# Second layer: normalised activations stored token tile by token tile, and a wider slot for the last head pair's projections

## The chip, the cores and the metric

The kernel runs on one core of one Trainium2 chip. The metric is the device time of one launch in microseconds; the time given for a kernel is the median over its runs. Engines are called as the profile calls them: PE is TensorE's matmul stream (PEld its weight loads), DVE is VectorE, ACT is ScalarE, POOL is GpSimd and SP is SyncE, which here issues nearly all DMAs.

## What is computed

Two transformer-like layers over 1024 latent tokens and 256 context tokens, width 1024. The first layer is grouped-query attention with rotary positions. The second, which the change touches, is neighbourhood attention: each query sees an 8 x 16 window of the 16 x 64 grid plus all context tokens. Cut to the second layer, the reference is:

```
hx = rms_norm(x, g) * (1 + scale_x) + shift_x        # 1024 latent tokens
hc = rms_norm(ctx, g) * (1 + scale_c) + shift_c      # 256 context tokens
q, k, v, z = split(hx @ w_in)                        # 16 heads of 64
kc, vc = split(hc @ w_in[:, k and v columns])
s = [q . k(window) / 8 + bias,  q . kc / 8]
p = softmax(s)
y = (p . [v(window), vc] * silu(z)) @ w_out
x = x + gate * y
return rms_norm(x, final_g)
```

Activations and weights are each held as a pair of half-precision tiles, a high part and a low part (`hb_hi`, `hb_lo`; `wb[u][0]`, `wb[u][1]`), and every projection is the sum of three products: high by high, high by low, low by high.

## The kernel before, in words

**Tiling.** Tokens come in ten tiles of 128: tiles 0 to 7 are latent, 8 and 9 context. The contraction over 1024 channels is eight chunks of 128, counted by `kt`. The 16 heads are worked on as eight pairs, u = 0 to 7.

**From the first to the second layer.** `a_out(t)` is the first layer's output projection of token tile t (matmuls into `poa`, line 1233) and adds it to the residual `x1s[t]`, called x10 to x17 in the listings. `b_ln(t)` calls `ln_tile`: sum of squares on ACT (`xj`, line 614), inverse root on POOL (`rs_ln`, line 607), scaling of the tile on DVE (line 616), eight transposes on PE into `plb{t}0` and `plb{t}1` (line 621), scale and shift on ACT into `tf` (line 625), and on DVE the copy to `hb_hi` (line 628) and the remainder to `hb_lo` (line 629). Both have the shape [128, 8 chunks, 1280 tokens]; one call of lines 628 and 629 writes four chunks of 128 tokens each.

**Per head pair.** `b_load(u)` fetches and splits the weights (`wb`). `b_qk(u)` makes five blocks of Q or K: 24 matmuls each into `pb{u}{which}{first token}` (which is 0 for Q and 1 for K), with weights as the stationary operand and 512 or 256 tokens of `hb` as the moving one (line 1319). ACT and DVE then evict them to `bq` and `bk` (lines 1332 to 1337). `b_vz(u)` makes V and the gate z for two token tiles at a time in `pvz{u}{0..4}`, with `hb` as the stationary operand (lines 1351 and 1354; `pvz{u}4` is the context's V), evicted to `bv` and `bsz`. `b_att(u)` computes window scores (`bsn{u}{head}{tile}`, lines 1382 and 1383) and context scores (`bsc`), adds the bias table `tb` and takes the maximum on DVE (line 1402), four exponentials per query tile on ACT (lines 1420 to 1423), the low part on POOL or DVE, a DMA transpose to `bpht`, and then the product with V into `bpv` (lines 1431 and 1433). `b_out(t)` is the final output projection (`pob{t}{half}`, line 1523), whose weights are `wob`.

**PSUM.** `pb`, `pvz` and the first four tiles' `pob` share two banks (tag `pj`), so a block can start when the last but one has been evicted. Window scores share two banks (`st`) with the later `pob`.

**What sets the order.** The program is first written out by `timeline`, which merges generators by a start and an end on a common axis: attention of pair u has the slot u to u + 1, the projections of pair u + 1 the slot u + BP0 to u + BP1, that is u to u + 0.95. Then `Planner` reorders every engine's instructions: it builds a dependency graph, runs a list schedule with its own costs, derives due times and reschedules, and the order it ends with is fixed per engine. To find what depends on what it does not use exact access patterns. `box` reduces each operand to one interval of elements per partition, from its first to its last element:

```
for s, c in ap[1:]:
    if s >= 0:
        ext += s * (c - 1)
return t, p0, p0 + ap[0][1] - 1, f0 + lo, f0 + ext, False
```

With [128, 8, 1280], the write of tile 6 into chunks 0 to 3 is the interval from element 768 to 3 x 1280 + 895, which holds the elements of tiles 0 to 3 in chunks 1, 2 and 3 as well.

Of the kernel before, what the change touches and what calls it, by code (L numbers as in the profile page):

```python
# [13 lines left out]
F16 = mybir.dt.float16  # L14
BF16 = mybir.dt.bfloat16
AF = mybir.ActivationFunctionType
ALU = mybir.AluOpType
# [4 lines left out]
P = 128  # L22
D = 1024
KT = D // P
NX = 8
NC = 2
NT = NX + NC
TOK = NT * P
# [10 lines left out]
BP0, BP1 = 0, 0.95  # L39
# [415 lines left out]
def timeline(items):  # L455

    live = [[g, float(a), (float(b) - a) / tot, 0.0] for g, a, b, tot in items]
    while live:
        it = min(live, key=lambda e: e[1] + e[2] * e[3])
        try:  # L460
            c = next(it[0])
            it[3] += c
            yield c
        except StopIteration:
            live.remove(it)


def once(f):
    f()
    yield 1.0  # L470
# [8 lines left out]
def trunk_kernel(ctx, tc, x, cx, cc, norm_g, b_cols, sel_c, w_mod, b_mod, a_w_in, a_qg, a_kg, a_w_out,  # L479
                 b_w_in, rpb, b_w_out, fin_g, cos_t, sin_t, mask_q, out):  # L480
    nc = tc.nc
    V, S, G, T, DM = nc.vector, nc.scalar, nc.gpsimd, nc.tensor, nc.sync
# [6 lines left out]
    def ps_pj(name, dt=F32, shape=(P, 512)):  # L489
        return psum.tile(list(shape), dt, name=name, tag="pj", bufs=2)  # L490

    def ps_mx(name, dt=F32, shape=(P, 512)):
        return psum.tile(list(shape), dt, name=name, tag="mx", bufs=2)
# [109 lines left out]
    def rstd_from(pool, ss, n, mul, add, tag):  # L603
        ms = pool.tile([P, 8], F32, name="ms_" + tag, tag="ms" + tag, bufs=2)
        V.tensor_scalar(ms[:, 0:n], ss, mul, add, op0=ALU.mult, op1=ALU.add)
        rs = pool.tile([P, 8], F32, name="rs_" + tag, tag="rs" + tag, bufs=2)
        G.tensor_tensor(rs[:, 0:n], ms[:, 0:n], mhalf[:, 0:n], op=ALU.pow)
        return rs

    def ln_tile(pool, xt, l, s, hi, lo, c0, nm):  # L610

        jk = pool.tile([P, D], BF16, name="xj" + nm, tag="xj", bufs=1)
        ss = pool.tile([P, 1], F32, name="lss" + nm, tag="lss", bufs=2)
        S.activation(jk, xt, AF.Square, accum_out=ss)
        rs = rstd_from(pool, ss, 1, 1.0 / D, EPS, "ln")
        V.tensor_scalar_mul(xt, xt, rs[:, 0:1])
        for hf in range(2):
            ps = ps_mx(f"pl{nm}{hf}", shape=(P, 4, P))
            for j in range(4):
                kt = hf * 4 + j  # L620
                T.transpose(ps[:, j, :], xt[:, kt * P:(kt + 1) * P], idf)
            tf = pool.tile([P, 4, P], F32, name=f"tf{nm}{hf}", tag="tf", bufs=2)
            for j in range(4):
                kt = hf * 4 + j
                S.activation(tf[:, j, :], ps[:, j, :], AF.Identity, scale=acol[l][:, kt, s:s + 1],
                             bias=scol[l][:, kt, s:s + 1])
            k4 = slice(hf * 4, hf * 4 + 4)
            V.tensor_copy(hi[:, k4, c0:c0 + P], tf)
            V.tensor_tensor(lo[:, k4, c0:c0 + P], tf, hi[:, k4, c0:c0 + P], op=ALU.subtract)
            yield 450  # L630

    def load_w(wt, src_ap, kt0, nk, width, nm):
# [244 lines left out]
    NPAIR = NH // 2  # L877
# [308 lines left out]
    items = a_proj(0, -first)  # L1186
# [17 lines left out]
    gts, x1s, ops = {}, {}, {}  # L1204
# [47 lines left out]


    bpool = ctx.enter_context(tc.tile_pool(name="bpool", bufs=1))
    hb_hi = bpool.tile([P, KT, TOK], F16, name="hb_hi")
    hb_lo = bpool.tile([P, KT, TOK], F16, name="hb_lo")
    tc.swap_default_side()
    lnpool = ExitStack()
    lnp = lnpool.enter_context(tc.tile_pool(name="lnpool", bufs=1))
    tc.swap_default_side()  # L1260

    def b_ln(t):
        yield from ln_tile(lnp, x1s[t], 1, 0 if t < NX else 1, hb_hi, hb_lo, t * P, f"b{t}")


    bq = ctx.enter_context(tc.tile_pool(name="bq", bufs=2))
# [6 lines left out]
    for r in range(GR):  # L1273
        a = bass.AP(rpb.tensor, rpb.offset + 15 - r, [[31 * 31, NH], [31, 31], [1, GR]])
# [7 lines left out]
    hb = (hb_hi, hb_lo)  # L1282
# [23 lines left out]
    def b_qk(u):  # L1306
        wt = wb[u]
        q1 = bq.tile([P, 2, NX * P], F16, name=f"bq1{u}", tag="q1")
        k1_ = bq.tile([P, 2, TOK], F16, name=f"bk1{u}", tag="k1")
        q2 = q2z[u % 2]  # L1310
        v1_ = bq.tile([P, NT, 2, P], F16, name=f"bv1{u}", tag="v1")
        sz = bq.tile([P, NX, P], F32, name=f"bsz{u}", tag="sz")
        bpairs[u] = (q1, q2, k1_, v1_, sz)
        for which, c0, n in ((0, 0, 512), (1, 0, 512), (1, 1024, 256), (0, 512, 512), (1, 512, 512)):
            ps = ps_pj(f"pb{u}{which}{c0}")
            m = 0
            for kt in range(KT):
                for a, b in ((0, 0), (0, 1), (1, 0)):
                    T.matmul(ps[:, 0:n], wt[a][:, kt, which * P:(which + 1) * P], hb[b][:, kt, c0:c0 + n],  # L1319
                             start=m == 0, stop=m == 3 * KT - 1)  # L1320
                    m += 1
                    if m % 3 == 0:
                        yield 640 * n / 512


            for i in range(2):
                own, oth = slice(i * 64, i * 64 + 64), slice(64 - i * 64, 128 - i * 64)
                src = ps[own, 0:n]
                cs = slice(c0, c0 + n)
                if which == 0:  # L1330
                    sc = HD ** -0.5 / WS
                    S.activation(q1[own, i, cs], src, AF.Copy, scale=sc)
                    V.scalar_tensor_tensor(q2[own, i, cs], src, sc, q1[own, i, cs], op0=ALU.mult, op1=ALU.subtract)
                    V.tensor_copy(q1[oth, i, cs], q1[own, i, cs])
                else:
                    S.activation(k1_[own, i, cs], src, AF.Copy, scale=1.0 / WS)
                    V.scalar_tensor_tensor(k1_[oth, i, cs], src, 1.0 / WS, k1_[own, i, cs], op0=ALU.mult,  # L1337
                                           op1=ALU.subtract)

    def b_vz(u):  # L1340
        wt = wb[u]
        v1_, sz = bpairs[u][3:5]
        for b in range(NT // 2):
            ps = ps_pj(f"pvz{u}{b}", shape=(P, 2, 2, P))
            for j in range(2):
                t = 2 * b + j
                m = 0
                for kt in range(KT):
                    for a, w in ((0, 0), (0, 1), (1, 0)):
                        if b < NX // 2:  # L1350
                            T.matmul(ps[:, :, j, :], hb[a][:, kt, t * P:(t + 1) * P], wt[w][:, kt, 256:512],  # L1351
                                     start=m == 0, stop=m == 3 * KT - 1)
                        else:
                            T.matmul(ps[:, 0, j, :], hb[a][:, kt, t * P:(t + 1) * P], wt[w][:, kt, 256:384],  # L1354
                                     start=m == 0, stop=m == 3 * KT - 1)
                        m += 1
                        if m % 3 == 0:
                            yield 320
            for j in range(2):
                vv = ps[:, 0, j].rearrange("p (h d) -> p h d", d=HD)  # L1360
                S.copy(v1_[:, 2 * b + j, :, 0:HD], vv)
                V.tensor_tensor(v1_[:, 2 * b + j, :, HD:P], vv, v1_[:, 2 * b + j, :, 0:HD], op=ALU.subtract)
            if b < NX // 2:
                th = bq.tile([P, 2 * P], F32, name=f"bth{u}{b}", tag="th", bufs=1)
                zf = ps[:, 1].rearrange("p t f -> p (t f)")
                S.activation(th, zf, AF.Tanh, scale=0.5 / WS)
                V.scalar_tensor_tensor(sz[:, 2 * b:2 * b + 2].rearrange("p t f -> p (t f)"), th, 1.0, zf,
                                       op0=ALU.add, op1=ALU.mult)
# [90 lines left out]
    C_BP, C_BA = 23040 + 25600, 8 * 1890 + 500  # L1459

    def b_proj(u):
        return timeline([(b_qk(u), 0, 0.6, 23040), (b_vz(u), 0.3, 1, 25600)])

    def steps(txt):
        for step in txt.split():
# [3 lines left out]
            else:  # L1469
# [4 lines left out]
    run_all(steps("l0 o8 l1 o9 l2 o4 l3 l8 o50 l9 o60 l4 o70"))  # L1474
    items = [(steps("o51 o61 l5 o71 l6 l7"), 0, 0.8, 5120 * 3 + 450 * 6), (b_load(0), 0.05, 0.6, 8),
             (b_qk(0), 0.85, 1.8, 23040)]
    run_all(timeline(items))
    lnpool.close()
# [8 lines left out]
    for h in range(2):  # L1487
        b_table(h)
    run_all(timeline([(b_vz(0), 0, 1, 25600), (b_load(1), 0, 0.5, 8)]))
    items = []  # L1490
    for u in range(NPAIR):
        items.append((b_att(u), u, u + 1, C_BA))
        if u + 1 < NPAIR:
            items.append((b_proj(u + 1), u + BP0, u + BP1, C_BP))
            for i in range(2):
                items.append((once(lambda h=2 * (u + 1) + i: b_table(h)), u + (0.76, 1.1)[i], u + 2, 1))
        if u + 2 < NPAIR:
            items.append((b_load(u + 2), u + 0.5, u + 0.95, 8))
# [112 lines left out]
```

## Time and profile before

| | |
|---|---|
| median of 3 runs | 1415.17 us (1411.48 to 1416.53) |
| the profiled execution's own time | 1411.77 us |
| its span, first to last instruction | 1410.0 us |
| PE busy | 1352.2 us, 96% of the span |
| DVE, ACT, POOL busy | 988.8, 957.4, 661.7 us |
| mean granted TensorE clock | 0.995 |
| second layer's first projection matmul (`pb`) | 798.2 us |
| second layer's first V and z matmul (`pvz`) | 830.5 us |
| first output projection matmul (`pob`) | 1295.5 us |

A row of the timeline reads: start in us, duration, engine, line, operation, output <- inputs, shapes, count of merged instructions, and in brackets how long the engine had been idle and what released it. Names there leave out the trailing numbers that the listings below have. Matmuls are pipelined: a 512-column matmul is shown with 0.38 us, but the next one starts about 0.22 us after it. A row of the windows reads: the stretch, its length, then busy us and count of PE, PEld, DVE, ACT and POOL, the granted clock, the DMA engines' mean busy share and GB/s.

### The profile page before, as it was taken

How to read it: one execution, taken by the hardware profiler on the slowest of the kernel's cores; microseconds unless marked ns; L12 is line 12 of the kernel's file. 1: busy time of each engine (PE TensorE's matmuls, PEld its weight loads, DVE VectorE, ACT ScalarE, POOL GpSimd, SP SyncE). 2: the span in 40 equal slices, each digit the busy share in tenths (PEclk: the TensorE clock that was granted, in tenths of full speed). 3: DMA queues.
4: the chain of work that ended last, by engine and by line, in shares of the span. 5: the costliest groups of instructions: out<-in, count | busy, mean ns of one | idle time of the engine just before them, and what ended most of it. 6: DMA issues, size and time to landing. Idle time of an engine off the chain costs nothing.

```text
span 1410.0 us, 35562 instructions
## 1 busy us (share of the span) xinstructions
PE 1352.2 (96%) x13458; PEld 941.4 (67%) x13458; DVE 988.8 (70%) x2564; ACT 957.4 (68%) x2354; POOL 661.7 (47%) x907
## 2 busy tenths in 40 slices
PE   5899999999999999999999899999999999999897
PEld 2457777777777777776555466767777776767443
DVE  3696887878898767688234735786777867687833
ACT  2553889898978787788634625677777867777821
POOL 2322678786877686678852201323222222223332
PEclk9999999999999999999999999999999999999999
DMA  9843567888866222245023414566756767577932
GB/s 262 241 130 94 97 119 148 142 162 164 151 126 125 50 75 50 68 118 166 23 90 105 143 36 113 93 144 133 128 113 121 145 106 160 97 152 139 190 110 105
DMA packets 412403, 173.98 MB, mean 123 GB/s; under 512 B 319012, under 2 KB 391364, under 8 KB 412232
## 3 DMA queue, kind: packets, MB, share of 16 engines
q1 hardware_dynamic: 411656, 171.68, 55.3%
q8 instruction: 105, 1.72, 0.5%
q14 instruction: 66, 0.54, 0.1%
q10 hardware_dynamic: 576, 0.03, 0.0%
HBM read 85.65 MB, written 12.06 MB: 69 GB/s over the span
## 4 chain that ended last, share of the span: by engine, by line
PE 75%; DVE 8%; ACT 7%; DMA 5%; issue 2%; POOL 2%; SPq 0%; DVEq 0%; POOLq 0%; ACTq 0%
PE pvz L1351 12%; PE pa L914 11%; PE pb L1319 9%; PE poa L1233 7%; PE pob L1523 5%; PE st L1141 3%; PE st L1140 3%; PE pkv L800 3%; DMA qpp<-qpp 3%; PE pm L944 2%; PE pv L1012 2%; PE pv L1013 2%; PE pv L1011 2%; PE bpv L1431 1%; PE pvz L1354 1%
## 5 line engine op out<-in xcount | busy, mean ns | idle before, releaser
L1005 POOL TENSOR_TENSOR pl<-pf,ph 128x256 f16<-128x256 f32 x400 | 283.5, 731 | 72.0 <-ACT pf L1127 54.1
L1005 POOL TENSOR_TENSOR bph<-bpf,bph 128x256 f16<-128x256 f32 (+1 forms) x128 | 100.9, 799 | 339.8 <-ACT bpf L1422 285.5
L914 PE MATMUL pa<-wa,x 128*128 128x256 f16 x1536 | 225.3, 274 | 3.1 <-DVE q16q L730 2.9
L1319 PE MATMUL pb<-hb_hi,wb 128*128 128x512 f16 (+1 forms) x640 | 193.8, 359 | 0.0
L1125 ACT ACTIVATE ph<-st 128x512 f16<-128x512 f32 x240 | 143.9, 602 | 64.1 <-PE st L1141 58.4
L1351 PE MATMUL pvz<-wb,hb_hi 128*128 128x256 f16 x1024 | 173.5, 273 | 4.5 <-DVE bk L1337 3.9
L914 PEld LDWEIGHTS <-x 128*128 128x128 f16 x1536 | 140.1, 98 | 37.0 <-DVE q16q L730 2.8
L945 DVE TENSOR_REDUCE mxp<-pm 128x1 f32<-128x512 f32 x192 | 128.6, 683 | 34.9 <-PE pm L944 34.1
L1127 ACT ACTIVATE pf<-st 128x512 f32<-128x512 f32 x240 | 144.4, 604 | 0.4
L1319 PEld LDWEIGHTS <-wb 128*128 128x128 f16 x960 | 92.9, 98 | 72.4 <-issue 1.1
L1351 PE MATMUL pvz<-wb,hb_lo 128*128 128x256 f16 x512 | 139.5, 273 | 0.0
L1012 PE MATMUL pv<-v,ph 128*128 128x64 f16 x960 | 123.5, 195 | 0.0
L1011 PE MATMUL pv<-v,ph 128*128 128x65 f16 x960 | 122.7, 193 | 0.0
L1013 PE MATMUL pv<-v,pl 128*128 128x65 f16 x960 | 121.3, 192 | 0.3 <-POOL pl L1005 0.3
L1351 PEld LDWEIGHTS <-hb_hi 128*128 128x128 f16 x1024 | 98.7, 98 | 25.3 <-issue 6.6
L1319 PE MATMUL pb<-hb_lo,wb 128*128 128x512 f16 (+1 forms) x320 | 114.7, 359 | 0.0
L1005 POOL TENSOR_TENSOR qpp<-qpf,qpp 128x256 f16<-128x256 f32 (+1 forms) x158 | 91.8, 605 | 42.7 <-ACT qpf L1083 38.1
L1011 PEld LDWEIGHTS <-ph 128*128 128x128 f16 x960 | 90.9, 97 | 21.4 <-issue 0.4
L1012 PEld LDWEIGHTS <-ph 128*128 128x128 f16 x960 | 90.5, 97 | 16.4
L1013 PEld LDWEIGHTS <-pl 128*128 128x128 f16 x960 | 91.1, 99 | 7.8 <-POOL pl L1005 1.0
L1233 PE MATMUL poa<-woa,oa 128*128 128x512 f16 x384 | 92.0, 379 | 0.0
L1140 PE MATMUL st<-q,k 128*128 128x512 f16 x240 | 90.7, 379 | 0.8 <-ACT pf L1127 0.6
(266 smaller groups left out, 3691.1 us busy)
## 6 DMA issues: line engine op xcount, KB each, us to landing
wg<-in_w_mod SPq DMA_DIRECT2D x64, 256.0 KB, 3.4
wsb<-in_b_w_in SPq DMA_DIRECT2D x64, 256.0 KB, 3.5
wm<-in_w_mod SPq DMA_DIRECT2D x32, 256.0 KB, 5.1
wsa<-in_a_w_in SPq DMA_DIRECT2D x64, 128.0 KB, 2.6
xstage<-in_x SPq DMA_DIRECT2D x8, 512.0 KB, 8.1
wsoa<-in_a_w_out SPq DMA_DIRECT2D x16, 256.0 KB, 2.8
x<-in_x SPq DMA_DIRECT2D x8, 512.0 KB
x_d<-x SPq DMA_DIRECT2D x8, 512.0 KB, 3.8
```

Of the source, the lines that this page charges most:

```text
L914: T.matmul(ps[:, :, i, :], hA(a, kt, t), wt[w][:, kt, :], start=n == 0, stop=n == 3 * KT - 1)
L945: V.tensor_reduce(mxs[i][:, t, ch:ch + 1], pm, axis=AX.X, op=ALU.max)
L1005: G.tensor_tensor(lo[:, c], p32[:, c], hi[:, c], op=ALU.subtract)
L1011: T.matmul(pv[:, t, :], hi[:, c], v[:, 0:65], start=first and t == 0, stop=False)
L1012: T.matmul(pv[:, t, 0:HD], hi[:, c], v[:, 65:129], start=False, stop=False)
L1013: T.matmul(pv[:, t, :], lo[:, c], v[:, 0:65], start=False, stop=last and t == n - 1)
L1125: S.activation(ph, st, AF.Exp)
L1127: S.activation(p32, st, AF.Exp)
L1140: T.matmul(so, k1[:, g, kc], q1[:, :, i, :], start=True, stop=False)
L1233: T.matmul(ps, lhs(a, kt), w[b][:, kt, :], start=n == 0, stop=n == 3 * KT - 1)
L1319: T.matmul(ps[:, 0:n], wt[a][:, kt, which * P:(which + 1) * P], hb[b][:, kt, c0:c0 + n], start=m == 0, stop=m == 3 * KT - 1)
L1351: T.matmul(ps[:, :, j, :], hb[a][:, kt, t * P:(t + 1) * P], wt[w][:, kt, 256:512], start=m == 0, stop=m == 3 * KT - 1)
```

## The change

Two edits. The first turns `hb_hi` and `hb_lo` from [128, chunk, token] into [128, token tile, chunk, 128 tokens]. `ln_tile` now gets one tile's block and writes four chunks that lie side by side. `b_qk` reads four (or two) tiles at one chunk, that is runs of 128 elements, 1024 elements apart, and its PSUM output is viewed in the same way; `b_vz` reads one tile at one chunk, as before. The number of instructions and the elements of each stay as they were. The second edit makes the slot of the last pair's projections, which are merged with the attention of pair 6, longer by 0.3: from 6 to 7.25 instead of 6 to 6.95.

```
-    def ln_tile(pool, xt, l, s, hi, lo, c0, nm):
+    def ln_tile(pool, xt, l, s, hi, lo, nm):
...
-            V.tensor_copy(hi[:, k4, c0:c0 + P], tf)
-            V.tensor_tensor(lo[:, k4, c0:c0 + P], tf, hi[:, k4, c0:c0 + P], op=ALU.subtract)
+            V.tensor_copy(hi[:, k4], tf)
+            V.tensor_tensor(lo[:, k4], tf, hi[:, k4], op=ALU.subtract)
...
-    hb_hi = bpool.tile([P, KT, TOK], F16, name="hb_hi")
-    hb_lo = bpool.tile([P, KT, TOK], F16, name="hb_lo")
+    hb_hi = bpool.tile([P, NT, KT, P], F16, name="hb_hi")
+    hb_lo = bpool.tile([P, NT, KT, P], F16, name="hb_lo")
...
-                    T.matmul(ps[:, 0:n], wt[a][:, kt, which * P:(which + 1) * P], hb[b][:, kt, c0:c0 + n],
+                    T.matmul(ps[:, 0:n].rearrange("p (t q) -> p t q", q=P), wt[a][:, kt, which * P:(which + 1) * P],
+                             hb[b][:, c0 // P:(c0 + n) // P, kt],
                              start=m == 0, stop=m == 3 * KT - 1)
...
-                            T.matmul(ps[:, :, j, :], hb[a][:, kt, t * P:(t + 1) * P], wt[w][:, kt, 256:512],
+                            T.matmul(ps[:, :, j, :], hb[a][:, t, kt], wt[w][:, kt, 256:512],
...
-            items.append((b_proj(u + 1), u + BP0, u + BP1, C_BP))
+            items.append((b_proj(u + 1), u + BP0, u + BP1 + 0.3 * (u == NPAIR - 2), C_BP))
```

Since the planner's intervals change with the layout, the order of instructions changes too. Up to about 775 us of the profile no row of any engine moves. Lines from 1320 on have a number higher by one after the change.

The first place is PE at the passage between the layers. `poa71` is the first layer's last output block; `pb000` and `pb010` are the first Q and K block of pair 0, `plb60` to `plb71` the transposes of normalised tiles 6 and 7. Before:

```order
L1319 MATMUL pb010_14642<-hb_hi_13857,wb00_14419 128x512
L1319 LDWEIGHTS wb00_14419
L1319 MATMUL pb010_14642<-hb_lo_13858,wb00_14419 128x512
L1319 LDWEIGHTS wb01_14420
L1319 MATMUL pb010_14642<-hb_hi_13857,wb01_14420 128x512
L621 MATMUL plb60_14551<-idf_66,x16_14298 128x128 x4
L621 MATMUL plb61_14563<-idf_66,x16_14298 128x128 x4
L621 MATMUL plb70_14583<-idf_66,x17_14360 128x128 x4
L621 MATMUL plb71_14595<-idf_66,x17_14360 128x128 x4
L1319 LDWEIGHTS wb00_14419
L1319 MATMUL pb000_14611<-hb_hi_13857,wb00_14419 128x512
```

Six projection matmuls stand ahead of the transposes (three of `pb000`, three of `pb010`, all at chunk 0), and the transposes of both tiles follow each other. After the change, around tile 7's transposes:

```order
L1319 MATMUL pb010_14642<-hb_hi_13857,wb00_14419 128x512
L621 MATMUL plb70_14583<-idf_66,x17_14360 128x128 x4
L1319 LDWEIGHTS wb00_14419
L1319 MATMUL pb010_14642<-hb_lo_13858,wb00_14419 128x512
L621 MATMUL plb71_14595<-idf_66,x17_14360 128x128 x4
L1319 LDWEIGHTS wb01_14420
L1319 MATMUL pb010_14642<-hb_hi_13857,wb01_14420 128x512
```

Tile 6's transposes now follow nine matmuls of `pb000`, and tile 7's come after 22 more: the other 15 of `pb000` and seven of `pb010`.

The second place is ACT a little later, where it finishes tile 7 (`tfb70`, `tfb71`), splits the next pair's weights (`wb10`) and evicts the first K block. Before:

```order
L625 ACTIVATE tfb71_14600<-plb71_14595,scol1_100,acol1_98 128x128
L638 ACTIVATE wb10_14783<-wsb16_14907 128x512
L625 ACTIVATE tfb71_14600<-plb71_14595,scol1_100,acol1_98 128x128
L638 ACTIVATE wb10_14783<-wsb17_14934 128x512
L1332 ACTIVATE bq10_14607<-pb000_14611 64x512 x2
L1336 ACTIVATE bk10_14608<-pb010_14642 64x512 x2
```

After:

```order
L625 ACTIVATE tfb70_14588<-plb70_14583,scol1_100,acol1_98 128x128
L1337 ACTIVATE bk10_14608<-pb010_14642 64x512
L625 ACTIVATE tfb71_14600<-plb71_14595,scol1_100,acol1_98 128x128
L638 ACTIVATE wb10_14783<-wsb16_14907 128x512
L638 ACTIVATE wb10_14783<-wsb17_14934 128x512
L1337 ACTIVATE bk10_14608<-pb010_14642 64x512
```

The evictions of `pb000` and `pb010` moved ahead of and between the last pieces of tile 7, and the two halves of the K block's eviction have three other instructions between them. On DVE likewise three stand between the two halves.

The third place is PE at the end of the last pair's projections. Before, the last V block and then the first scores of pair 7:

```order
L1354 MATMUL pvz74_21816<-wb70_20449,hb_lo_13858 128x128
L1431 LDWEIGHTS bpht614_21724
L1431 MATMUL bpv611_21664<-bv16_20041,bpht614_21724 128x128
...
L1382 MATMUL bsn700_22005<-bk17_21029,bq17_21028 128x256
L1383 LDWEIGHTS bq21_13866
L1383 MATMUL bsn700_22005<-bk17_21029,bq21_13866 128x256
```

After, the same scores and then the third V block:

```order
L1383 MATMUL bsn700_21903<-bk17_21029,bq17_21028 128x256
L1384 LDWEIGHTS bq21_13866
L1384 MATMUL bsn700_21903<-bk17_21029,bq21_13866 128x256
...
L1384 MATMUL bsc700_21935<-bk17_21029,bq21_13866 128x256
L1352 LDWEIGHTS hb_hi_13857
L1352 MATMUL pvz72_21691<-wb70_20449,hb_hi_13857 128x2x128
```

Before, all of `pvz72`, `pvz73` and `pvz74` stand ahead of the first score of pair 7. Now the scores of its first two query tiles stand ahead of all three blocks, those of the next two (`bsn702`, `bsn703`, `bsc702`) within `pvz74`, and the first `pob00` follows instead of preceding `bsn710`. The products of the last part of pair 6 (`bpv611`) are spread among them. Elsewhere all engines have exchanges of near neighbours in the attention of pairs 0 and 1 and of the first half of pair 2, and again from the attention of pair 6 on; in between the rows are as before.

More of the change, by code (lines that the diff above doesn't have):

```diff
@@ L1262, in b_ln @@
     def b_ln(t):
-        yield from ln_tile(lnp, x1s[t], 1, 0 if t < NX else 1, hb_hi, hb_lo, t * P, f"b{t}")
+        yield from ln_tile(lnp, x1s[t], 1, 0 if t < NX else 1, hb_hi[:, t], hb_lo[:, t], f"b{t}")
     bq = ctx.enter_context(tc.tile_pool(name="bq", bufs=2))
@@ L1350, in b_vz @@
                         if b < NX // 2:
-                            T.matmul(ps[:, :, j, :], hb[a][:, kt, t * P:(t + 1) * P], wt[w][:, kt, 256:512],
+                            T.matmul(ps[:, :, j, :], hb[a][:, t, kt], wt[w][:, kt, 256:512],
                                      start=m == 0, stop=m == 3 * KT - 1)
                         else:
-                            T.matmul(ps[:, 0, j, :], hb[a][:, kt, t * P:(t + 1) * P], wt[w][:, kt, 256:384],
+                            T.matmul(ps[:, 0, j, :], hb[a][:, t, kt], wt[w][:, kt, 256:384],
                                      start=m == 0, stop=m == 3 * KT - 1)
```

## The prediction

> **What bounds the kernel now.** I read the page's busy times first, then the windows, then the timeline of the two windows in which PE is not full.
>
> ```profile
> span 1410.0 us, 35562 instructions
> PE 1352.2 (96%) x13458; PEld 941.4 (67%) x13458; DVE 988.8 (70%) x2564; ACT 957.4 (68%) x2354; POOL 661.7 (47%) x907
> ```
>
> PE is the bound: 58 us of the span are all that it leaves open. A change that removes no matmul can only win part of that. The windows of the second layer show where it lies; the second number is the length, the third PE's busy time.
>
> ```profile
> 800.00:820.00 20.00, 15.57 (x85) 9.37 (x85) 15.58 (x28) 13.08 (x30) 4.04 (x7) 0.91 0.51 157
> 820.00:840.00 20.00, 20.00 (x138) 13.29 (x136) 6.18 (x15) 3.86 (x9) 1.05 (x2) 1.00 0.00 1
> ...
> 860.00:1260.00 400.00, 394.39 (x3627) 290.13 (x3626) 294.54 (x841) 292.62 (x849) 103.25 (x138) 1.00 0.65 129
> ...
> 1300.00:1320.00 20.00, 15.24 (x133) 8.76 (x131) 17.31 (x53) 20.00 (x61) 7.30 (x9) 1.00 0.96 188
> 1320.00:1340.00 20.00, 18.69 (x132) 10.05 (x133) 15.43 (x46) 14.16 (x45) 8.24 (x9) 1.00 1.03 203
> 1340.00:1360.00 20.00, 20.00 (x134) 10.44 (x132) 7.73 (x21) 4.21 (x11) 5.58 (x5) 1.00 0.36 108
> ```
>
> Two holes: 4.43 us at 800 to 820, with the granted clock down to 0.91, and 4.76 + 1.31 = 6.07 us at 1300 to 1340, where ACT is busy for 20.00 of 20 us. Between them PE misses 5.6 us in 400, so whatever PE gains early is kept there: it runs on its own work, not on another engine's pace. Both holes are where the order changes.
>
> **First hole, the passage between the layers.** Rows of the timeline:
>
> ```profile
> 795.79 1.04 PE L621 MATMUL plb<-idf,x 128*128 128x128 f32 x8
> 798.18 0.38 PE L1319 MATMUL pb<-hb_hi,wb 128*128 128x512 f16 x1
> 798.99 0.74 DVE L616 TENSOR_SCALAR x<-x,rs_ln 128x1024 f32<-128x1024 f32 x1
> 799.88 1.06 PE L621 MATMUL plb<-idf,x 128*128 128x128 f32 x8 [0.24 <-DVE x L616]
> 804.48 0.74 DVE L616 TENSOR_SCALAR x<-x,rs_ln 128x1024 f32<-128x1024 f32 x1
> 805.37 1.91 PE L621 MATMUL plb<-idf,x 128*128 128x128 f32 x8 [4.43 <-DVE x L616]
> 807.07 1.06 PE L1319 MATMUL pb<-hb_hi,wb 128*128 128x512 f16 x2
> 807.92 0.63 PE L1319 MATMUL pb<-hb_lo,wb 128*128 128x512 f16 x1
> 808.35 0.84 PE L1319 MATMUL pb<-hb_hi,wb 128*128 128x512 f16 x2
> 809.02 0.38 PE L1319 MATMUL pb<-hb_lo,wb 128*128 128x512 f16 x1
> 809.24 0.59 PE L1319 MATMUL pb<-hb_hi,wb 128*128 128x512 f16 x2
> 809.67 0.38 PE L1319 MATMUL pb<-hb_lo,wb 128*128 128x512 f16 x1
> ```
>
> PE stands at tile 7's transposes until DVE has normalised tile 7 (805.2), although the matmuls queued behind them read only tiles 0 to 3. Full pace is three 512-column matmuls in 809.67 - 809.02 = 0.65 us, 0.216 each. After the stall PE is slow: eight transposes take 1.91 us instead of 1.06, and from 807.07 to 809.02 five matmuls take 1.95 us instead of 1.08.
>
> Removed: the wait at tile 6's transposes, 0.24 us, since nine instead of six matmuls precede them (798.18 + 9 x 0.216 = 800.1, and tile 6 is ready at 799.7). Removed: the wait at tile 7's, 4.43 us. PE then leaves tile 6's transposes at 800.1 + 1.06 = 801.2, and the 22 matmuls ahead of tile 7's last 4.75 us, to 805.9; tile 7, whose chain through ACT, POOL and DVE starts at the last first-layer block and doesn't move, is ready at 805.2. Without the stall the slow stretch goes too: 1.91 - 1.06 = 0.85 and 1.95 - 1.08 = 0.87 us. Sum: 0.24 + 4.43 + 0.85 + 0.87 = 6.39 us.
>
> By the Trainium skill, "TensorE: Matmul & The Clock Gate", Part 1, the array's clock halves after an idle window of about 3.4 us and comes back after a busy one, and these windows run free. The 4.43 us stall with 0.427 us per matmul behind it agrees. By the page the slow stretch needn't follow in every run; the sum would then be 4.67 us instead of 6.39.
>
> Added: evictions. The second Q block needs the bank of the first K block. Before, that passed like this:
>
> ```profile
> 817.21 0.59 ACT L1336 ACTIVATE bk<-pb 64x512 f16<-64x512 f32 x1 [2.39 <-PE pb L1319]
> 819.18 0.69 DVE L1337 SCALAR_TENSOR_TENSOR bk<-pb,bk 64x512 f16<-64x512 f32 x1 [0.66 <-ACT bk L1336]
> 820.17 0.38 PE L1319 MATMUL pb<-hb_hi,wb 128*128 128x512 f16 x1
> ```
>
> The eviction took 2.66 us (817.21 to 819.87) and PE came 0.3 us after it. Now the two halves of it have three other instructions between them on ACT and on DVE. On DVE these are two pieces of tile 7 and one weight split; with a split at 0.68 us and a piece at 0.41 to 0.69, as rows here show, DVE is done about 0.5 us after PE would like to start. I take 0.5; the bounds are 0 (all hidden) and 2.7 us (the whole eviction bare). Behind the waiting Q block nothing on PE could run, as the queue is in order; the next V blocks wait for it.
>
> ```profile
> 811.74 0.42 DVE L628 CAST hb_hi<-tfb 128x512 f16<-128x512 f32 x1
> 812.07 0.68 DVE L639 SCALAR_TENSOR_TENSOR wb<-wsb,wb 128x512 f16<-128x512 f32 x1
> 812.67 0.68 DVE L629 TENSOR_TENSOR hb_lo<-tfb,hb_hi 128x512 f16<-128x512 f32 x1
> 813.44 0.55 SPq L1289 DMA_DIRECT2D tb<-tabd  x1
> 820.15 0.42 DVE L1402 CUSTOM_DVE_ANT_1 bpf<-bsn,tb 128x256 f32<-128x256 f32 x1 [0.28 <-POOL tb L1291]
> ```
>
> On the queue of SP the bias table's fetch waits for tile 7's last piece (813.35, then 813.44), and the first score's DVE step comes 6.7 us later. I expect tile 7's last piece about 2 us later than now, at some 815.3. DVE then stands at the first score from 816 to 822 while the second Q block's eviction queues behind it. I cost this at nothing: PE has the second Q and K block to do, 48 matmuls at 0.216 = 10.4 us from 814, so it asks for the bank only at 824.5. If that cover fails it is 1 us. First hole: 6.39 - 0.5 = 5.9 us.
>
> **Layout itself.** The moving operand of `pb` becomes four runs of 128 elements. The first layer's scores already read their moving operand so (line 1140), with the same duration:
>
> ```profile
> L1319 PE MATMUL pb<-hb_hi,wb 128*128 128x512 f16 x508 | 169.2, 381 | 0.0
> L1140 PE MATMUL st<-q,k 128*128 128x512 f16 x240 | 90.7, 379 | 0.8 <-ACT pf L1127 0.6
> ```
>
> So nothing is added; the bound is -2 to +2 ns per matmul, times 960 about 2 us either way, and I take 0. The forty pieces of lines 628 and 629 now write one run; they lie on DVE, nearly all beside the `poa` matmuls with which PE is full, 0 as well.
>
> **Second hole, the last pair.** The order puts `pvz72` to `pvz74` behind the first scores of pair 7. Who waits for what from 1295 to 1340 on PE, and on ACT from 1280, and two groups of ACT from 1297 to 1320:
>
> ```profile
> PE bsn L1382 <- DVE bmx L1402: 2.4, 4, 0.9
> PE pob L1523 <- DVE wob L639: 1.2, 3, 0.6
> PE bpv L1431 <- DVE boc L1447: 0.7, 1, 0.7
> PE bpv L1431 <- DMA bpht<-bph: 0.6, 2, 0.4
> PE pob L1523 <- ACT wob L638: 0.5, 1, 0.5
> PE bsc L1382 <- ACT bpf L1423: 0.5, 1, 0.5
> ...
> ACT bph L1420 <- DVE bnx L1412: 3.2, 2, 2.4
> ACT bv L1361 <- PE pvz L1351: 2.2, 1, 2.2
> ...
> L1421 ACT ACTIVATE bph<-bsc,bnx 128x256 f16<-128x256 f32 x10 | 4.9, 506 | 0.0
> L638 ACT ACTIVATE wob<-wsob 128x512 f16<-128x512 f32 x7 | 4.8, 683 | 0.0
> ```
>
> PE's six waits make 5.9 us. All say that exponentials and maxima come too slowly once no projection is left to fill PE; while PE ran the last projections, ACT stood idle for lack of scores (2.2 us at once). The new order gives ACT two query tiles' exponentials during those projections, and takes their share out of the stretch behind. ACT's demand there: from 1297 to 1320, 23 us without a gap, it does ten query tiles (one context exponential of line 1421 each) and seven `wob` splits for 4.8 us, so a tile takes (23 - 4.8) / 10 = 1.8 us; two tiles less are 3.6 us less. PE's work there shrinks by less, ten score matmuls (about 1 us). So PE's 4.2 us of waits (5.9 - 1.2 - 0.5) for scores, maxima and V can shrink by 3.6 - 1 = 2.6 us for the two tiles; a further 1.1 I give for pair 6's last V products (`bpv611`), which are spread among the projections now and free banks and DVE earlier. The 1.7 us for `wob` stay, as ACT still does the splits between exponentials. I take 3.7 us, with 0 and 5.9 as bounds. Past 1340 PE is full and the tail is not touched.
>
> **Small exchanges** in pairs 0 to 2: the 5.6 us in 400 are all that they can win; about half of that stretch is reordered. I take 0, plus or minus 1.5.
>
> **Sum.** -5.9 - 3.7 + 0 = -9.6 us against the profiled execution's 1411.77: 1402.2. That execution lies 3.4 us under the median of 1415.17, so against the median 1405.6.
>
> **The rivals.**
>
> *Only the first hole closes.* ACT is full at 1300 to 1320 whatever stands on PE, and its backlog still holds the last pair; the filler moved there is used up before. For it: ACT's 20.00 of 20, and the next scores (`bsn702`) stand late within `pvz74`, so ACT idles once more while PE runs the V blocks. Against: two tiles are certainly done sooner. Gives 1415.2 - 5.9 = 1409.3.
>
> *The first hole doesn't close.* If the matmuls now put ahead themselves wait for tile 6 or 7, the stall only moves to them. Against: `pb000` and `pb010` read tiles 0 to 3 alone, which stand in DVE's order ahead of tile 5's scaling. Gives 1415.2 - 3.7 = 1411.5.
>
> *Slower: the four runs cost PE time.* One cause, 960 matmuls of `pb`. It has to eat 9.6 us and 7.1 more, so it decides at 16.7 / 960 = 17 ns per matmul, 8% of the 216 ns pace; with 30 ns it gives 1405.6 + 28.8 = 1434. Against it stand line 1140's 379 ns.
>
> *Slower in the end part:* the V of the context tokens (`pvz74`) comes later, and every `bpv7` needs it; its eviction sits on ACT behind pair 7's third tile. It starts to matter if ACT gets to it later than the 4.2 us that PE's score, V and `pob` matmuls cover (some 13 `pob` at 0.216 and 1.4 us others). Three or four us too late gives 1409; to lose 16.7 us it would have to hold half the attention part, for which nothing speaks.
>
> **How the numbers follow.** A difference under 0.5%, 7.1 us, is about what a measurement of this kernel can't tell from none. Forecast, both holes: 0.66, range 1401 to 1409. Only the first: 0.16. Only the second: 0.07. Strided read slower: 0.04. End part late: 0.04, mostly near no change. Another way: 0.03. Faster by over 7.1 us (under 1408.1) holds most of the forecast (0.60) and the lower edge of the first rival (0.05): 0.65. Slower: 0.04 + half of the last two cases, 0.08. The rest, 0.27, is the same. The range goes from both holes fully closed plus exchanges (1415.2 - 6.4 - 5.9 - 1.5 = 1401.4, and 2 lower for the spread of the runs) to the case in which only the second closes and an exchange loses, 1412.
>
> **What would show it.** First: no wait of `plb` for line 616 over 0.5 us, a granted clock of 1.00 at 800 to 820, PE over 19 of 20 us there, and the first `pvz` matmul about 6 us earlier. Second: PE's sum of waits over the last pair under 2.5 us, and the first `pob` followed by no idle over 0.5. Layout: line 1319's 512-column form at 379 to 382 ns. It is wrong if a new wait of `pb` for line 1337 or of `bpv` for line 1362 of several us stands in the list, or ACT is full in more windows of the last pair than now.

## The result and the profile after

The changed kernel takes 1404.75 us (median; 1402.74 to 1406.13), the kernel before 1414.21 beside it: ratio 0.9933, 95% interval 0.991 to 0.9955. In a second comparison the same pair gave 0.995 (0.9933 to 0.9967). By the medians the change is worth 9.5 and 6.3 us. The profiled execution took 1404.96 us.

```profile
span 1403.2 us, 35558 instructions
PE 1349.2 (96%) x13458; PEld 939.5 (67%) x13458; DVE 991.8 (71%) x2564; ACT 958.2 (68%) x2354; POOL 660.6 (47%) x907
```

PE's busy time fell by 3.0 us and its idle time by 3.8, with the same 13458 matmuls. The windows in which the holes were (columns as in the prediction):

```profile
800.00:820.00 20.00, 19.00 (x110) 10.82 (x109) 17.44 (x31) 14.46 (x33) 3.31 (x4) 1.00 0.50 152
...
860.00:1260.00 400.00, 394.22 (x3647) 290.82 (x3646) 297.16 (x853) 294.92 (x854) 102.97 (x138) 1.00 0.68 129
1300.00:1320.00 20.00, 16.58 (x153) 10.22 (x152) 18.82 (x58) 19.57 (x58) 6.04 (x8) 1.00 1.04 183
1320.00:1340.00 20.00, 20.00 (x148) 10.56 (x147) 11.66 (x32) 10.42 (x34) 9.13 (x9) 1.00 0.73 167
```

At 800 to 820 PE went from 15.57 to 19.00 us and the granted clock from 0.91 to 1.00; the middle is as it was; at 1300 to 1340 PE gained 2.65 us, though the kernel is some 4 us ahead there, so that these two windows don't hold quite the same work; the stages below do. Rows of PE's timeline at the first hole, those in between left out:

```profile
796.72 1.04 PE L621 MATMUL plb<-idf,x 128*128 128x128 f32 x8
801.04 1.04 PE L621 MATMUL plb<-idf,x 128*128 128x128 f32 x8
806.67 0.60 PE L621 MATMUL plb<-idf,x 128*128 128x128 f32 x4
807.32 0.60 PE L621 MATMUL plb<-idf,x 128*128 128x128 f32 x4
815.54 0.39 PE L1319 MATMUL pb<-hb_hi,wb 128*128 128x512 f16 x1 [1.00 <-DVE bk L1338]
825.91 0.38 PE L1352 MATMUL pvz<-wb,hb_hi 128*128 128x256 f16 x2
```

No transpose has a bracket any more; in its place stands one wait of 1.00 us for the eviction of the first K block. PE's waits in the last pair follow, split where its projections end (the last `pvz` matmul ends at 1293.19 before and at 1294.20 after). While the projections still run, before (1243 to 1290) and after (1239 to 1295):

```profile
PE pvz L1351 <- DVE bk L1337: 0.8, 1, 0.8
```
```profile
PE bsn L1383 <- DVE bmx L1403: 1.2, 3, 0.6
PE pvz L1352 <- DVE bsz L1368: 0.8, 1, 0.8
PE pvz L1352 <- DVE bk L1338: 0.3, 1, 0.3
PE bpv L1432 <- DMA bpht<-bph: 0.2, 1, 0.2
```

Behind them, after (1295 to 1345); before, it is the list of the prediction, 5.9 us:

```profile
PE bsn L1383 <- DVE bmx L1403: 1.2, 2, 0.9
PE bpv L1432 <- DMA bpht<-bph: 0.9, 1, 0.9
PE pob L1524 <- DVE bmx L1403: 0.7, 1, 0.7
PE pob L1524 <- DVE wob L639: 0.6, 1, 0.6
```

So the waits behind the projections fell from 5.9 to 3.4 us, and those beside them rose from 0.8 to 2.5. In all, PE's waits from 1240 to 1340 make 6.7 us before and 5.8 after.

**Where the time went, by stages.** Profiled executions start up to some us apart (tile 5's transposes stand at 795.79 before and at 796.72 after, before anything has changed), so I cut the timelines at marks on PE: A from tile 5's transposes to the first `pvz`, B to pair 6's context K block (the 256-column `pb`), C to pair 7's, D to the end. All in us, from the start of the first matmul at each mark:

| kernel | A | B | C | D |
|---|---|---|---|---|
| before | 34.74 | 350.83 | 62.50 | 166.09 |
| after | 29.19 | 350.81 | 63.03 | 163.43 |
| after, second time | 29.21 | 351.04 | 63.03 | 163.11 |
| layout alone | 29.17 | 350.70 | 62.49 | 166.00 |
| slot alone | 34.70 | 351.30 | 63.04 | 163.57 |
| old layout, new order | 29.17 | 350.78 | 62.49 | 165.64 |
| new layout, old order | 34.60 | 350.55 | 62.49 | 166.00 |

After minus before: -5.55, -0.02, +0.53, -2.66: together -7.7 us. A belongs to the layout edit alone, C and D nearly all to the slot alone, and they add: in A, C and D the layout alone gives -5.7, the slot alone -2.0, both -7.7.

### The profile page after: what moved, and what is told of

Same layout as the page of the kernel before. It is cut to its first block, busy times and chain, and to the rows that moved or that the text cites. A ratio compares the mean times of both kernels' runs of the same rounds, so it can differ in the third digit from the quotient of the medians.

```text
span 1403.2 us, 35558 instructions
## 1 busy us (share of the span) xinstructions
PE 1349.2 (96%) x13458; PEld 939.5 (67%) x13458; DVE 991.8 (71%) x2564; ACT 958.2 (68%) x2354; POOL 660.6 (47%) x907
## 3 DMA queue, kind: packets, MB, share of 16 engines
q8 instruction: 105, 1.72, 0.5%
## 4 chain that ended last, share of the span: by engine, by line
PE 75%; DVE 9%; DMA 5%; ACT 5%; POOL 3%; issue 3%; SPq 0%; POOLq 0%; DVEq 0%; ACTq 0%
PE pvz L1352 12%; PE pa L914 11%; PE pb L1319 9%; PE poa L1233 7%; PE pob L1524 5%; PE pkv L800 3%; PE st L1140 3%; PE st L1141 3%; PE pm L944 2%; DMA qpp<-qpp 2%; PE pv L1012 2%; PE pv L1013 2%; PE pv L1011 2%; PE bpv L1432 2%; PE pvz L1355 1%
```

## The experiments

**The two edits apart, and the layout apart from its order.** First the new layout with the old slot:

```
-            items.append((b_proj(u + 1), u + BP0, u + BP1 + 0.3 * (u == NPAIR - 2), C_BP))
+            items.append((b_proj(u + 1), u + BP0, u + BP1, C_BP))
```

> The new layout with the old slot (6 to 6.95). Theory (the gain is PE's stall at tile 7's transposes, the clock that falls behind it, and a smaller part from the slot): about 5.5 us under before, 1408.7, and in the profile no wait of plb for line 616 over 0.5 us, while the last pair's waits stay near 5.9 us. Rival (the slot makes most of it): within 2 us of before.

Measured: 1406.6 us, ratio 0.9954 (0.994 to 0.9968). Then the old layout with the longer slot:

> The old layout with the wider slot for the last pair's projections. Theory: 2 us under before (the last stretch of the two profiles differs by 2.2), at most the 3.7 us predicted, with the 4.4 us wait of plb still there. Rival (the slot's gain only exists once PE comes early from the first hole): no difference from before.

Measured: 1411.25 us, ratio 0.9991 (0.9977 to 1.0004), which by itself can't be told from no change; the stages show its 2.0 us in C and D.

The layout edit does two things: it changes what PE and DVE read and write, and it changes the intervals by which the planner orders. Two kernels give each without the other. The old layout, where `box` hands the planner the intervals of the new one:

```
+        if t.name.startswith("hb_"):
+            lo, hi = f0 + lo, f0 + ext
+            k0, c0 = divmod(lo, TOK)
+            k1, c1 = divmod(hi, TOK)
+            return t, p0, p0 + ap[0][1] - 1, (c0 // P * KT + k0) * P, (c1 // P * KT + k1) * P + P - 1, False
```

> The old layout and the old slot, but the planner is given intervals for hb as if it were stored token tile by token tile; every engine's order is then that of the layout alone. Theory (only the order counts): the same as the layout alone, about 5.5 us under before. Rival (the layout itself speeds or slows the copies, the reads or the waits that are compiled in): like before, 1414, or as far from the layout alone as the rows' reading costs.

And the new layout, where `box` hands it the old intervals:

> The new layout and the old slot, but the planner is given the intervals that hb had before; every engine's order is then that of before. Theory: equal to before within 1.5 us, with the 4.4 us wait of plb back, and line 1319's 512-column form at 379 to 382 ns. Rival (four runs of 128 elements cost PE time, hidden in the result by a larger gain): slower than before by 5 us or more. Rival (layout itself gains): faster by some us.

Measured: 1406.53 us, ratio 0.9951 (0.9934 to 0.9967), and 1413.44 us, ratio 0.9998 (0.9984 to 1.0011). In the traces PE, DVE, ACT and POOL run their instructions in the order of the layout alone in the first, and in the order of the kernel before in the second. The order makes the whole gain; the layout makes none that these runs can tell, with an interval of about 2 us either way. Rows of the second of them (new layout, old order), from the timeline and from the groups; its lines are shifted by four:

```profile
800.21 1.07 PE L625 MATMUL plb<-idf,x 128*128 128x128 f32 x8 [0.24 <-DVE x L620]
805.70 1.94 PE L625 MATMUL plb<-idf,x 128*128 128x128 f32 x8 [4.43 <-DVE x L620]
```
```profile
L1323 PE MATMUL pb<-hb_hi,wb 128*128 128x512 f16 x512 | 170.4, 380 | 0.0
```

The stall is back in full with the slow transposes behind it, and `pb` reading four runs of 128 takes 380 ns. In the changed kernel it takes 379, and in the old layout with the new order, which reads one run of 512, also 379:

```profile
L1319 PE MATMUL pb<-hb_hi,wb 128*128 128x512 f16 x512 | 171.0, 379 | 1.0 <-DVE bk L1338 1.0
```
```profile
L1324 PE MATMUL pb<-hb_hi,wb 128*128 128x512 f16 x512 | 169.7, 379 | 1.0 <-DVE bk L1342 1.0
```

The ends of matmuls are modelled, so I also took the starts: from one 512-column matmul of `pb` to the next start on PE it is 216 ns (median) in all of these kernels and in the kernel before.

**Both edits once more,** to see whether they add:

> The changed kernel once more. If the two edits only add, the ratio is that of the layout alone (0.9954) less what the slot alone gave (0.0009): 0.9945, or 1405.0 us against 1412.8. If the longer slot is worth more once the first hole is closed (theory: the stretch before it is then less disturbed), it stays at the 0.993 measured first, 1403 us, two us under the layout alone. If the first figure was spread of the runs, it comes out at 0.9945.

Measured: 1407.27 us, ratio 0.995 (0.9933 to 0.9967). The sum of both, 0.9945, lies well within the interval and the first 0.9933 at its edge. With the stages, which add, I read this as: they add, and the first 0.9933 was partly spread.

**Is the slow stretch behind the stall the stall's own?** Into the kernel before, work was put that fills most of the stall:

```
-            ps = ps_mx(f"pl{nm}{hf}", shape=(P, 4, P))
+            ps = ps_mx(f"pl{nm}{hf}", shape=(P, 4, P)); [T.transpose(d[:, 0:P], idf, idf) for d in ([ps_st("dm0"), ps_st("dm1")] if nm == "b7" and hf == 0 else []) for _ in range(16)]
```

> Kernel before, with 32 transposes of the identity matrix put on PE into two free window-score banks: 17 ahead of tile 6's transposes and 15 right behind them, 0.133 us each, 4.3 us in all; no other instruction moves. The work fills the 4.7 us in which PE stood, and nothing can start earlier. Theory of the prediction: the slow stretch (0.85 + 0.87 us) follows from PE standing still, so it goes although the stall's length remains: tile 7's eight transposes take 1.06 instead of 1.91 us, three projection matmuls behind them 0.65 us, the granted clock at 800 to 820 is 1.00, and the time falls by 1.7 us (ratio 0.9988), in which case the layout's 6.5 us are 4.7 of standing, 1.7 of slow clock, less the new wait. Rival: the slow rows come from something else at this place (ACT and DVE reading the same banks); then they stay, with no change of the time (1.000).

Measured: 1409.01 us, ratio 0.9977 (0.9964 to 0.999): faster than before, with 32 matmuls more. One thing moved that the expectation did not allow for: the six projection matmuls that stood ahead of tile 6's transposes now stand behind them and help to fill the stall; all other instructions keep their order. PE's timeline, and its window 800 to 820:

```profile
801.36 2.02 PE L618 MATMUL dm<-idf 128*128 128x128 f32 x17
803.21 1.04 PE L621 MATMUL plb<-idf,x 128*128 128x128 f32 x8
804.09 1.80 PE L618 MATMUL dm<-idf 128*128 128x128 f32 x15
...
808.55 1.06 PE L621 MATMUL plb<-idf,x 128*128 128x128 f32 x8 [1.36 <-DVE x L616]
809.45 0.59 PE L1319 MATMUL pb<-hb_hi,wb 128*128 128x512 f16 x2
809.88 0.38 PE L1319 MATMUL pb<-hb_lo,wb 128*128 128x512 f16 x1
...
811.17 0.38 PE L1319 MATMUL pb<-hb_lo,wb 128*128 128x512 f16 x1
```
```profile
800.00:820.00 20.00, 18.57 (x116) 11.55 (x114) 16.41 (x29) 15.39 (x37) 2.62 (x3) 1.00 0.51 160
```

Tile 7's transposes take 1.06 us, not 1.91, and from their start to the third `hb_lo` product it is 811.17 - 808.55 = 2.62 us, where before it was 809.67 - 805.37 = 4.30: 1.68 us less, against 1.72 expected. Stage A takes 33.31 us, 1.43 less than before. The medians differ by 4.6 us, more than these rows explain; the interval, 1.4 to 5.1 us, holds both. A pause of 1.36 us leaves the clock at 1.00; one of 4.43 us took it to 0.91. This agrees with the idle window of about 3.4 us that the Trainium skill gives in "TensorE: Matmul & The Clock Gate", Part 1. Pauses in the runs with `wob` on POOL, at the end of this section, agree with it only in part.

**How far the slot may reach.** Half of it, 0.15:

> The changed kernel with the last pair's slot longer by 0.15 instead of 0.3, that is to 7.1. If the gain of the second edit comes from query tiles that get done during the projections, half the reach gives about half of it: PE's waits from 1240 to 1340 between those of the layout alone (6.9 us listed) and those of the changed kernel (about 5.8), ratio 0.9942. Rival: the longest reach is past the best, and the waits it adds at 1243 to 1278 are what it pays; then 0.15 is as good or better (0.993 or less).

Measured: 1409.01 us, ratio 0.9963 (0.9947 to 0.998). Stage D is 166.14 us, as without the edit, and PE's waits from 1240 to 1340 make 6.8 (those of the layout alone make 6.7, not the 6.9 of the expectation):

```profile
PE pob L1524 <- DVE wob L639: 1.8, 3, 1.1
PE bpv L1432 <- DMA bpht<-bph: 1.5, 3, 0.6
PE bsn L1383 <- DVE bmx L1403: 1.5, 3, 0.7
PE bsc L1383 <- ACT bpf L1424: 1.1, 2, 0.6
PE pob L1524 <- DVE bmx L1403: 0.9, 1, 0.9
```

Half the reach gives nothing that shows in the time, so the gain is not in proportion to it, and neither theory fits. The work did move by half: behind the last `pvz` matmul ACT has 16 context exponentials (`bph` from `bsc`) left to do, where the layout alone has 18 and the changed kernel 14. But PE's waits from 1295 on are still 5.5 us (5.9 and 3.4 in those two). The same 0.3 for all pairs (the condition `* (u == NPAIR - 2)` taken out):

> The changed kernel with the slot of the projections 0.3 longer for all pairs, not only the last. If what PE lacks in the middle (5.6 us in 400, mostly V blocks that wait for evictions of K and scores that wait for maxima) is due to projections running out at the end of a slot, as in the last pair, PE's waits from 860 to 1260 fall from about 5 to 3 us and the ratio is 0.992. Rival: at a pair's end the next pair's first scores need Q and K of the same projections, so a longer slot only delays them; waits for Q or K appear and the ratio is 0.994 to 0.997. My estimate is 0.9930.

Measured: 1413.47 us, ratio 0.9992 (0.998 to 1.0004): the whole gain is lost. One step from pair to pair in the middle, of this kernel and then of the changed one, and PE's waits from 860 to 1260 in this kernel:

```profile
995.35:1059.86 64.51, 63.07 (x577) 45.83 (x576) 46.16 (x135) 45.82 (x135) 16.39 (x22) 1.00 0.66 126
```
```profile
987.20:1050.63 63.43, 62.19 (x579) 45.98 (x577) 46.83 (x136) 46.97 (x136) 16.25 (x22) 1.00 0.68 130
```
```profile
PE pb L1319 <- DVE bv L1363: 3.3, 6, 0.6
PE bsc L1383 <- ACT bpf L1424: 2.1, 6, 0.4
PE pvz L1355 <- DVE bq L1334: 1.4, 6, 0.2
```

This pair takes 1.1 us longer, and the four others between pair 2 and pair 7 take 1.1 to 1.7 us longer each. Once in every pair a Q or K block now waits for the eviction of a V block, where in the changed kernel a V block waits once for that of a K block (3.3 us in 6 waits there as well). In all, the listed waits of this stretch grew from 5.3 to 7.4 us. The rest of the loss is in waits too short for the list: from start to start, PE's matmuls lose another 0.9 us in each pair. My estimate of 0.9930 was wrong; the rival named such waits, though it put the ratio at 0.994 to 0.997. What the last pair needs, the others don't.

**Is ACT's load what the last pair waits for?** `wob`'s high parts moved from ACT to POOL, in the changed kernel and in the layout alone:

```
-        S.activation(h, st, AF.Copy, scale=WS)
+        (G.tensor_scalar_mul(h, st, WS) if nm.startswith("ob") else S.activation(h, st, AF.Copy, scale=WS))
```

> The changed kernel with the high parts of wob (line 638, 16 instructions of 0.68 us in the last pair) made by POOL instead of ACT; POOL is idle there for half of the time. Measured from pair 7's context K block to the end, the kernel before and the layout alone take 166.0 us, the changed kernel 163.3. Theory of the prediction: what the last pair waits for is ACT's load; then ACT's relief by 4.8 us in 1288 to 1320 takes PE's waits there from 3.4 to about 1.5 us and the stretch to 161.5, ratio about 0.9928. Rival 1: it is the chain from a score over maximum and exponential to the transposed DMA, whose length doesn't depend on ACT's load; then 163.3 and 0.9940. Rival 2: POOL, which needs about 1.2 us for such an instruction by the 0.92 us of a 384-column one, gets wob ready later; then pob waits longer and it is 164 to 166.

> The new layout with the old slot and wob's high parts on POOL. PE's listed waits from 1240 to 1340 with the old slot are 6.9 us, and 166.0 us from pair 7's context K block to the end. If ACT's load is the shortage, its relief does what the longer slot does: waits of 4 us or less, 163.5 us, ratio 0.9938. If the shortage is that no filler is left on PE for a chain of fixed length, only the slot helps: 165.5 to 166, ratio 0.9954.

Measured: 1415.32 us, ratio 1.0017 (1.0003 to 1.003), and 1421.4 us, ratio 1.0065 (1.0052 to 1.0078). They lose about 10 and 15 us against the same kernels with `wob` on ACT, and don't answer the question, since the relief of ACT costs more elsewhere: in the first, from 1300 to 1320, ACT is busy for 12.93 us instead of 19.57, but POOL for 17.70 instead of 6.04, and PE's 16.12 are no more than the 16.58 of the changed kernel, which is some 6 us ahead there. Of the first of the two: POOL's group of line 638 from 1240 to 1350, DVE's of line 639 from 1228 to 1320, and PE's longest new wait; then DVE's line 639 in the changed kernel:

```profile
L638 POOL TENSOR_SCALAR wob<-wsob 128x512 f16<-128x512 f32 x11 | 16.6, 1528 | 8.6 <-PE pvz L1355 8.6
...
L639 DVE SCALAR_TENSOR_TENSOR wob<-wsob,wob 128x512 f16<-128x512 f32 x16 | 15.5, 969 | 3.5 <-POOL wob L638 3.5
```
```profile
PE pb L1319 <- DVE bq L1334: 3.2, 1, 3.2
```
```profile
L639 DVE SCALAR_TENSOR_TENSOR wob<-wsob,wob 128x512 f16<-128x512 f32 x16 | 11.0, 691 | 0.3 <-ACT wob L638 0.2
```

An instruction that takes ACT 0.68 us takes POOL 1.53, DVE stands 3.5 us for it, and DVE's own instruction grows from 0.69 to 0.97 us. The two halves of a Q block's eviction start on DVE at 1240.37 and 1244.90, with one of these instructions and several steps of the attention between them, and PE stands 3.2 us. The Trainium skill, "SBUF — State Buffer", section "Who interferes with whom", says that a DVE instruction with two inputs in SBUF and a GpSimd (POOL) instruction that reads SBUF contend with each other; line 639 has two such inputs, and the 0.28 us more agree with that.

**The new wait of 1.00 us.** The low parts of the last two pieces of pair 1's weights were moved from DVE to POOL, to take one of them out of DVE's way:

```
-        V.scalar_tensor_tensor(o, st, WS, h, op0=ALU.mult, op1=ALU.subtract)
+        if nm in ("b16", "b17"):
+            G.tensor_scalar_mul(st, st, WS)
+            G.tensor_tensor(o, st, h, op=ALU.subtract)
+        else:
+            V.scalar_tensor_tensor(o, st, WS, h, op0=ALU.mult, op1=ALU.subtract)
```

> The changed kernel with the low parts of the last two pieces of pair 1's weights (line 639, 0.68 us each) made by POOL in two steps each, so that one of them no longer stands on DVE between tile 7's pieces and the first K block's eviction. Theory: the new wait of the second Q block (1.00 us for line 1338) is this queue on DVE, and falls by the 0.68 us to about 0.3; the first pvz comes 95.3 us after the first plb instead of 96.0, and the ratio falls by 0.0005, which the times can't show. Rival: ACT's half of the eviction ends it; the wait stays at 0.8 to 1.0.

Measured: 1404.14 us, ratio 0.9945 (0.9928 to 0.9963), no different from the changed kernel. The wait is 1.5 us, not 0.3, and stage A 29.69. DVE's rows of that stretch in this kernel, and PE's wait:

```profile
816.73 0.69 DVE L629 TENSOR_TENSOR hb_lo<-tfb,hb_hi 128x512 f16<-128x512 f32 x1
817.34 0.83 DVE L628 CAST hb_hi<-tfb 128x512 f16<-128x512 f32 x1
818.21 0.69 DVE L629 TENSOR_TENSOR hb_lo<-tfb,hb_hi 128x512 f16<-128x512 f32 x1
818.93 1.14 DVE L1342 SCALAR_TENSOR_TENSOR bk<-pb,bk 64x512 f16<-64x512 f32 x2
```
```profile
PE pb L1323 <- DVE bk L1342: 1.5, 1, 1.5
```

The split is gone from DVE, but the planner put tile 7's last remainder (0.69 us) into its place, and the cast beside POOL's scaling takes 0.83 us instead of 0.42. Measured from tile 5's transposes, the second half of the eviction starts 0.5 us later, and PE's wait grows by 0.5. So it is DVE's queue that sets this wait, though the experiment didn't shorten it. Both moves together:

> The changed kernel with both moves to POOL. If both theories hold: 1.8 + 0.7 = 2.5 us less than the changed kernel, ratio 0.992. If neither: 0.994.

Measured: 1415.07 us, ratio 1.0021 (1.0007 to 1.0035), as `wob` on POOL alone. No version tried is clearly faster than the changed kernel.

The three kernels with `wob` on POOL also say more about the clock. In each of them PE waits for a Q block's eviction ahead of pair 7's context K block. That row of PE and its window, in the changed kernel with `wob` alone on POOL, and then with both moves:

```profile
1245.64 0.27 PE L1319 MATMUL pb<-hb_hi,wb 128*128 128x256 f16 x1 [3.18 <-DVE bq L1334]
1240.00:1260.00 20.00, 15.86 (x131) 11.10 (x130) 18.09 (x47) 14.64 (x42) 8.66 (x10) 1.00 0.64 150
1320.00:1340.00 20.00, 17.05 (x122) 9.75 (x122) 14.57 (x47) 17.32 (x54) 9.78 (x11) 0.83 0.76 149
```
```profile
1243.93 0.37 PE L1323 MATMUL pb<-hb_hi,wb 128*128 128x256 f16 x1 [3.18 <-DVE bq L1338]
1240.00:1260.00 20.00, 16.69 (x125) 11.88 (x124) 16.50 (x43) 14.33 (x42) 7.16 (x8) 0.83 0.61 137
```

The same pause of 3.18 us leaves the clock at 1.00 in one and takes it to 0.83 in the other. Nor does it take one long pause: in the first of the two the clock is 0.83 at 1320 to 1340 as well, where the longest of several pauses is 1.71 us. With `wob` on POOL in the layout alone the clock there is 0.67, so part of the 10 and 15 us is slow clock; how much was not taken apart. The Trainium skill, "TensorE: Matmul & The Clock Gate", Part 1, says that the windows run free. The two pauses of 3.18 us agree with that; the stall of 4.43 us doesn't show it, as all three traces that have it (before, slot alone, new layout with old order) have the slow transposes behind it.

## Why the prediction was right, and where its steps were off

The predicted 1405.6 us and the measured 1404.75 differ by less than the runs do among themselves. That they come so close is partly luck: the sum was 9.6 us, and the stages show 7.7. Step by step:

- **The stall of 4.43 us and the 0.24 us go.** Right: no transpose waits; stage A shows it with the layout alone, and with the order alone.
- **The slow stretch goes with them, 0.85 + 0.87 us.** Right, shown by the filled stall: 1.68 of 1.72 us. The 4.67 us that stood as the other possible sum would have been too little.
- **The new wait, 0.5 us (0 to 2.7).** It is 1.00. The mechanism and the place were right: on DVE, ahead of the eviction's second half, stand the two pieces of tile 7 and the weight split that were named. The term was too small by half a microsecond.
- **The first hole gives 5.9.** It gave 5.4 by these rows (6.39 - 1.00) and 5.55 by stage A. It is kept through the middle: B is the same within 0.02 us.
- **Tile 7 and the first score.** Tile 7's last piece was expected at some 815.3 us; it starts at 815.51, with PE's marks 0.9 us later. DVE then stands for 4.03 us at the first score, and it cost nothing, as said: from the end of the 1.00 us wait up to the first `pvz` no wait of PE is listed.

```profile
815.51 0.69 DVE L629 TENSOR_TENSOR hb_lo<-tfb,hb_hi 128x512 f16<-128x512 f32 x1
...
821.87 0.42 DVE L1403 CUSTOM_DVE_ANT_1 bpf<-bsn,tb 128x256 f32<-128x256 f32 x1 [4.03 <-POOL tb L1292]
```

- **The layout itself, 0 (within 2 us).** Right: 379 and 380 ns against 379, 216 ns from start to start, and a ratio of 0.9998 with the old order.
- **The second hole, 3.7 us (0 to 5.9).** This is the step that was off, though within its bounds. It gave 2.1 us (-2.66 in D, +0.53 in C, where three matmuls moved from D to C account for 0.43). The sum took 2.6 + 1.1 us off the 4.2 us of waits for exponentials, maxima and V behind the projections, left the 1.7 us for `wob`, and put the scores that move in among the projections at nothing. Behind the projections those 4.2 us fell to 2.8, by 1.4 instead of 3.7, and the waits for `wob`, which were to stay, fell from 1.7 to 0.6. The term that was missing is the one beside the projections: there the waits rose from 0.8 to 2.5 us, as scores now wait for maxima and V blocks for the evictions of others. This is steady: the changed kernel's second profile has 2.9 us beside and 3.1 behind, the slot alone 2.8 and 3.0, the layout alone 0.8 and 5.9 as before. Two signs that the prediction named for this hole did not come: waits under 2.5 us over the last pair, and no idle over 0.5 us behind the first `pob` (0.6 and 0.7 stand in the list).

  The listed waits thus fell by 0.9 us only. The whole 2.1 us show in the starts of PE's matmuls over C and D. Counted with the median time from start to start of their form, they need 210.0 us in both kernels, and what they lose besides falls from 9.4 to 8.2 us at the listed waits (each costs about 0.16 more than its listed length, and there are two fewer) and from 1.1 to 0.2 in waits too short for the list.

  ACT's share of the argument held: from the last `pvz` matmul to the last context exponential, ACT has 14 of these instead of 18 and is busy for 32.7 us instead of 40.0. That is the 1.8 us for each that the prediction took, for four of them instead of two. (The 2.2 us cited for ACT without scores were a wait for a V block.) But that this load is what holds the last pair was argued, and the runs didn't show it: at 1300 to 1320 ACT is still busy for 19.57 of 20 us, half the slot moved two of the four exponentials without a gain, and taking load off ACT brought a costlier queue on POOL and DVE. It stays open whether ACT or the chain from score to transposed probabilities sets the pace there.
- **Exchanges in pairs 0 to 2, 0 (within 1.5).** Right: B is 350.83 and 350.81.

The sum was 9.6 us and the stages show 7.7: 0.35 missing in the first hole, 1.57 in the second. The two timings (9.5 and 6.3 us between medians) lie on either side of that.

## What to carry to other kernels

Where a planner finds dependencies by intervals, a layout is also a statement about order: two kernels, one with each layout's intervals and the other's data, tell which of the two pays, and here it was the order alone, as far as the runs can tell. A stall is priced with the clock behind it: here 4.43 us of standing cost 1.7 us more in slow matmuls. Work moved into a full stretch isn't free there either: what the longer slot took off the end, it paid back in part as waits beside the projections. And an edit that helps at the end of a pipeline, where nothing follows, need not help in its middle: spread over all pairs it lost the whole gain.

## What the runs showed of the hardware that was not expected

Putting useless work into a stall made a kernel faster: 32 transposes and six moved matmuls where PE had stood for 4.7 us, ratio 0.9977 (0.9964 to 0.999). A pause of 3.18 us left the granted clock at 1.00 in one kernel and took it to 0.83 in another. And POOL is no free place for work that DVE or ACT does: its scaling of 128x512 took 1.53 us where ACT's took 0.68, DVE's instruction of the same stretch took 0.97 us instead of 0.69, and a cast beside such a scaling 0.83 instead of 0.42.
